# One hybrid decoder layer: the second MLP product summed before its gate, conditioning units dealt out by phase, attention probabilities scaled on ScalarE

## The chip, the cores and the metric

The kernel runs on one core of a Trainium2 chip. The metric is device time in microseconds, median of three runs. Engines are named as the profile names them: PE is TensorE (matmuls; PEld its weight loads), DVE is VectorE, ACT is ScalarE, SP is SyncE, whose queue issues nearly all DMAs.

## What is computed

One layer of a Griffin-like decoder on 256 tokens of width 2048, in float32, cut to what the change touches:

```python
mod = silu(c) @ w_ada + b_ada                     # 6 x 2048 conditioning values
shift1, scale1, gate1, shift2, scale2, gate2 = split(mod, 6)
h = rmsnorm(x) * norm1_g * (1 + scale1) + shift1
lru_x, lru_gate, q, k, v, g_a, g_b = split(h @ w_in)
...
e = exp(logits - m)                               # window 128, sink, 32 heads, 4 kv heads
p = e / (sum(e) + exp(sink - m))
o = p @ v
...
merged = sigmoid(g_a) * y_a + sigmoid(g_b) * y_b
x = x + gate1 * (merged @ w_out)
h2 = rmsnorm(x) * norm2_g * (1 + scale2) + shift2
x = x + gate2 * (relu(h2 @ w_ff1) ** 2 @ w_ff2)   # d_ff = 8192
return rmsnorm(x) * final_g
```

## The kernel before, in words

Everything is kept transposed: 128 features on the partitions, 256 tokens along the row. The work on TensorE is a list of units (`units`). One unit is one block of 128 output features, so up to 16 weight blocks of 128x128; `w_load` fetches its weights by one DMA of up to 1 MB into a `raw` tile (four of them, `RAW_BUFS`, line 260's conditioning rows use the same four), then `w_split` cuts them in chunks of 1024 columns into a rounded part `wh` (ACT, L160) and a remainder `wl` (DVE, L162), with three buffers of each. PE multiplies with both parts: three matmuls for each block in the narrow form (L176, L177, L178), two in the wide form (L189, L190, with a first one at L192). The loop at the end of the builder loads up to two units ahead (`LOOK`), runs a unit, and then takes work from two lists.

The first list is `side`: attention, the recurrence and elementwise work, put there by `later(cost, ...)` and paid from a credit of 2.3 per full unit. For four heads at a time `att_scores` does the score matmuls (L452), the bias, the row maximum (DVE, L457) and the exponentials in place, with their row sums (ACT, L467); `att_values` multiplies the exponentials by the reciprocal of the sum (DVE, L484, eight instructions for each group of four heads), transposes them on PE (L489), copies them out of PSUM (ACT, L491) and multiplies them with v (L496, copied out at L498). There are eight groups.

The second list is the conditioning. `mod` has 96 columns of 128 values; each is one `ada_unit`: a DMA of 1 MB from `w_ada` (SP) and one DVE instruction over 128x2048 with a running sum (L260). The first 32 (shift1, scale1) are done before the units begin. Of the rest 16 give gate1, 16 scale2, 16 shift2 and 16 gate2, in this order. `ada_credit` says when: during the input projection (units before `n_ya`) it grows by 0.45 for each 2048 columns of weights; from there to the unit `n_z`, in which 80 are wanted, by what is left over the units left; after that by 0.3 a unit. Whenever it is above zero one unit is issued and 1 is taken off. A unit of the second MLP product in the first quarter (`ff2_unit`, `c == 0`, L693) asks with `flush(5 * KT + f + 1)` for the column of gate2 that it needs.

The units in order: k and v (2 units of two blocks with 6 of their 16 weight blocks left, since the first ten were done in an earlier pass), q (8 such), the recurrence's x branch (8 such), its gate branch (2 such, then 12 of one block with 10 weight blocks left), the branch gates gA and gB (4 with 10 blocks, 28 full), the two branch projections (32 full), the output projection (16), and then four quarters of the MLP: 16 units of the first product (`ff1_unit`, L675 to L677), 16 of the second (`ff2_unit`). A result of a quarter of the first product is kept as a pair tile of the pool `kp` (49 pair tiles); `ff2_unit` multiplies the two PSUM halves by the column of gate2 and adds them to the residual `x1`, with one DVE instruction for each half, in every quarter. In the last quarter it also takes the squares for the final norm.

Instructions are put on the engines in an order that the Tile scheduler fixes at build time from priorities and modelled times; on the chip each engine takes its queue strictly in that order.

Of the kernel before, what the change touches and what calls it, by code (L numbers as in the profile page):

```python
# [19 lines left out]
KT = 16  # L20
# [13 lines left out]
LAG, CC, CG, CV, CS = 2, 1.0, 0.6, 0.3, 2.5  # L34

ADA_LAST, QUIET_OUT, QUIET_FF1 = 0.3, 2, 3
LOOK, CREDIT, Z_FROM, ADA_RATE, ADA_FIRST = 2, 2.3, 12, 0.45, 0.85

PASSES = [(0, 2, 56), (2, 6, 56), (6, 10, 40)]
NATIVE = {(2, u) for u in range(0, 56, 16)}  # L40
# [16 lines left out]
def hybrid_layer(ctx: ExitStack, tc: tile.TileContext, x, xt, wada, w_p, w_r, w_f, vec, lruw, relb,  # L57
# [19 lines left out]
    def pair(dt=F32):  # L77
        return kp.tile([P, 2, T], dt, tag="k2", name=nm("k"))
# [293 lines left out]
    def later(cost, fn, *a):  # L372
        side.append((cost, fn, a))
# [99 lines left out]
    def att_values(g):  # L473

        kv = g // 2
        ss, dn = ast.pop(g)
        vs = slice(64 * kv, 64 * kv + 64)
        for t in range(2):
            po = bank([P, T])
            pvs = []  # L480
            for i in (2 * t, 2 * t + 1):
                for b, sl in HALVES:
                    c = 2 * i + b
                    ve.tensor_scalar(out=ss[i][:, sl], in0=ss[i][:, sl], scalar1=dn[:, c:c + 1], scalar2=None,  # L484
                                     op0=ALU.mult)
                pt = bank([P, 384])

                for n, j in enumerate((0, 2, 1)):
                    te.transpose(pt[:, n * P:(n + 1) * P], ss[i][:, j * P:(j + 1) * P], idt)  # L489
                pv = tmp([P, 384])  # L490
                se.activation(pv, pt, AF.Copy)  # L491
                pvs.append(pv)

            for kb, cols, pc in ((1, slice(0, 256), slice(0, 256)), (0, slice(128, 256), slice(256, 384))):
                for i in range(2):
                    te.matmul(po[64 * i:64 * i + 64, cols], lhsT=vtok[:, kb, vs], rhs=pvs[i][:, pc],  # L496
                              start=kb == 1, stop=kb == 0)
            se.activation(res[F_Q + 2 * g + t], po, AF.Copy)  # L498
# [170 lines left out]
    def ff1_unit(c, f):  # L669
# [14 lines left out]
            ff[c, f] = split(t[:, 1])  # L684
        add_unit(run)

    def ff2_unit(c, f):
        def run(w):
            if c == 0:
                flush(5 * KT + f + 1)  # L690
            ps = gemm_wide(w, [ff[c, j] for j in range(16)], join=False)
            for i in range(2):
                ve.scalar_tensor_tensor(out=x1[f], in0=ps[:, i], scalar=mod[:, 5 * KT + f:5 * KT + f + 1], in1=x1[f],  # L693
                                        op0=ALU.mult, op1=ALU.add)
            if c == 3:
                if f == 0:
                    stat[3] = sp.tile([P, T], F32, tag="asq", name=nm("asq"), bufs=1)

                if f < 15:
                    sumsq(stat[3], x1[f], f == 0)  # L700
                else:
                    stat[4] = tmp([P, T])
                    se.activation(stat[4], x1[f], AF.Square)
                se.activation(x1[f], x1[f], AF.Copy, scale=vc[:, V_GF + f:V_GF + f + 1])
        add_unit(run)

    def flush(n_ada=0):
        while side:
            _, fn, a = side.pop(0)
            fn(*a)  # L710
        while ada_next[0] < n_ada:
            ada_unit()

# [3 lines left out]
    in_units(F_Q, 16, q_fin)  # L717
    in_units(F_LX, 16, lx_fin)
    in_units(F_LG, 16, lg_fin)
    in_units(F_GA, 16, lambda f, ps, part: branch_gate(F_GA + f, ps, part))  # L720
    in_units(F_GB, 16, lambda f, ps, part: branch_gate(F_GB + f, ps, part))
    n_ya = len(units)
# [15 lines left out]
    for n, (run, src, size, native) in enumerate(units):  # L738
# [11 lines left out]
            credit -= cost  # L750
        left = n_z - n
        if n < n_ya:
            ada_credit += size / 2048 * ADA_RATE
        else:
            ada_credit += max(0, 5 * KT - ada_next[0]) / left if left > 0 else ADA_LAST
        if n_ff1 - QUIET_OUT <= n < n_ff1 or n_ff1 + 16 - QUIET_FF1 <= n < n_ff1 + 16:
# [120 lines left out]
```

## Time and profile before

| | us |
|---|---|
| median of three runs (1599.3 to 1602.97) | 1599.39 |
| the profiled execution's own time | 1599.42 |
| its span, first to last instruction | 1597.6 |
| PE busy in the span | 1560.4 |
| DVE busy | 1223.7 |
| ACT busy | 872.7 |

The page gives the busy time of each engine over the whole span. The view of windows gives the same for any stretch, with the mean granted clock of TensorE and the rate of the DMAs; the view of waits gives the idle time of an engine and the instruction that ended it; the timeline gives single instructions in order of time. On PE an instruction's busy time is longer than its spacing, since matmuls are pipelined.

### The profile page before, as it was taken

Reading aid. Unit: us, or ns where it says so; the run is one execution under the profiler, and the core shown is the slowest. Engines: PE = TensorE matmul, PEld = TensorE weight load, DVE = VectorE, ACT = ScalarE, POOL = GpSimd, SP = SyncE. Lnnn points to the kernel's source line nnn. Section 1 sums busy time; section 2 is a strip of 40 time slices with the busy share of each in tenths; the row PEclk is TensorE's granted clock in tenths of the full one; section 3 lists DMA queues with packets and bytes.
Section 4 is the critical chain, followed back from the end, with each engine's and each line's share of the span. In section 5 each row is a group of like instructions: output and inputs, shape, how many; then the busy total and the mean of one; then the engine's idle time right before and its main releaser. Section 6 shows DMA issues by size and latency. Waiting matters only on the chain.

```text
span 1597.6 us, 26576 instructions
## 1 busy us (share of the span) xinstructions
PE 1560.4 (98%) x10684; PEld 1434.8 (90%) x10684; DVE 1223.7 (77%) x1970; ACT 872.7 (55%) x1421; POOL 0.2 (0%) x4
## 2 busy tenths in 40 slices
PE   5999999999999999999999999999999999999997
PEld 4999998899988888888889998899989998899987
DVE  7798998898989879788898667865665556655665
ACT  5733447686886564445465553355434553355554
POOL 0000000000000000000000000000000000000000
PEclk7999999999999999999999999999999999999999
DMA  8898976557767768787886666865555555555552
GB/s 322 325 345 324 338 272 208 201 191 238 287 237 280 265 244 310 277 297 292 323 302 245 237 237 243 332 242 185 185 184 185 185 185 184 185 185 185 185 186 78
DMA packets 61707, 387.99 MB, mean 243 GB/s; under 512 B 6576, under 2 KB 11024, under 8 KB 19216
## 3 DMA queue, kind: packets, MB, share of 16 engines
q1 hardware_dynamic: 57168, 381.95, 66.7%
q10 hardware_dynamic: 4416, 4.35, 0.9%
q8 instruction: 83, 1.36, 0.3%
q14 instruction: 40, 0.33, 0.1%
HBM read 384.13 MB, written 2.15 MB: 242 GB/s over the span
## 4 chain that ended last, share of the span: by engine, by line
PE 88%; DVE 5%; ACT 2%; DMA 2%; issue 2%; SPq 0%; ACTq 0%; DVEq 0%
PE pg L190 32%; PE pg L189 15%; PE pg L676 8%; PE pg L675 8%; PE pg L677 8%; PE pg L178 4%; PE pg L176 4%; PE pg L177 4%; DVE wl L162 2%; DMA ra<-in_wada_dram 1%; PE pg L205 1%; PE pg L192 1%; DVE ra L260 1%; ACT wh L160 1%; PE pa L489 1%
## 5 line engine op out<-in xcount | busy, mean ns | idle before, releaser
L160 ACT ACTIVATE wh<-rw 128x1024 fp32r<-128x1024 f32 (+2 forms) x534 | 545.4, 1024 | 612.4 <-PE pg L190 318.0
L162 DVE TENSOR_TENSOR wl<-rw,wh 128x1024 fp32r<-128x1024 f32 (+2 forms) x534 | 628.2, 1178 | 241.7 <-ACT wh L160 235.7
L190 PE MATMUL pg<-k,wh 128*128 128x512 f32 x2240 | 776.4, 396 | 0.3 <-DVE k L142 0.3
L189 PE MATMUL pg<-k,wl 128*128 128x256 f32 x2100 | 589.4, 281 | 0.2 <-DVE wl L162 0.2
L190 PEld LDWEIGHTS pg<-k,wh 128*128 128x128 f32 x2240 | 412.5, 188 | 86.4 <-PE pg L190 0.6
L189 PEld LDWEIGHTS pg<-k,wl 128*128 128x128 f32 x2100 | 397.0, 189 | 7.2 <-DVE wl L162 0.6
L676 PE MATMUL pg<-z,wh 128*128 128x256 f32 x1024 | 290.6, 284 | 0.0
L675 PE MATMUL pg<-z,wh 128*128 128x258 f32 x1024 | 289.7, 283 | 0.0
L677 PE MATMUL pg<-z,wl 128*128 128x258 f32 x1024 | 289.7, 283 | 0.0
L176 PE MATMUL pg<-k,wh 128*128 128x256 f32 x832 | 237.4, 287 | 10.9 <-ACT k L141 9.0
L178 PE MATMUL pg<-k,wl 128*128 128x256 f32 x832 | 234.0, 284 | 3.0 <-DVE wl L162 2.8
L177 PE MATMUL pg<-k,wh 128*128 128x256 f32 x832 | 235.1, 283 | 0.2 <-DVE k L142 0.2
L260 DVE CUSTOM_DVE_ANT_0 ra<-ra,scr,vc 128x2048 f32<-128x2048 f32 x96 | 225.1, 2346 | 12.1 <-DMA ra<-in_wada_dram 12.0
L677 PEld LDWEIGHTS pg<-z,wl 128*128 128x128 f32 x1024 | 195.3, 191 | 0.0
L675 PEld LDWEIGHTS pg<-z,wh 128*128 128x128 f32 x1024 | 195.1, 190 | 0.0
L676 PEld LDWEIGHTS pg<-z,wh 128*128 128x128 f32 x1024 | 194.3, 190 | 0.2
L176 PEld LDWEIGHTS pg<-k,wh 128*128 128x128 f32 x832 | 157.5, 190 | 13.9 <-ACT k L141 9.5
L178 PEld LDWEIGHTS pg<-k,wl 128*128 128x128 f32 x832 | 157.2, 190 | 5.2 <-DVE wl L162 4.0
L177 PEld LDWEIGHTS pg<-k,wh 128*128 128x128 f32 x832 | 157.8, 190 | 1.2 <-DVE k L142 0.5
L693 DVE SCALAR_TENSOR_TENSOR k<-pg,mod,k 128x256 f32<-128x256 f32 x128 | 61.8, 484 | 31.3 <-PE pg L190 29.2
L192 PE MATMUL pg<-k,wl 128*128 128x256 f32 x140 | 39.6, 283 | 2.1 <-DVE wl L162 2.1
L679 DVE TENSOR_REDUCE sh<-pg 128x1 f32<-128x2 f32 x64 | 10.2, 159 | 38.4 <-PE pg L677 38.4
(154 smaller groups left out, 983.5 us busy)
## 6 DMA issues: line engine op xcount, KB each, us to landing
rw<-in_w_f_dram SPq DMA_DIRECT2D x204, 1024.0 KB, 4.9
ra<-in_wada_dram SPq DMA_DIRECT2D x96, 1024.0 KB, 6.2
rw<-in_w_p_dram SPq DMA_DIRECT2D x31, 1024.0 KB, 6.0
rw<-in_w_r_dram SPq DMA_DIRECT2D x20, 768.0 KB, 4.9
rw<-in_w_r_dram SPq DMA_DIRECT2D x16, 640.0 KB, 3.9
bt<-ud ACTq DMA_DIRECT2D x8, 512.0 KB, 4.2
xt<-in_xt_dram SPq DMA_DIRECT2D x8, 256.0 KB, 5.0
lw<-in_lruw_dram SPq DMA_DIRECT2D x4, 512.0 KB, 5.7
```

The source lines that it names most:

```text
L160: se.activation(wh[:, :c], raw[:, o:o + c], AF.Copy)
L162: ve.tensor_tensor(out=wl[:, :c], in0=raw[:, o:o + c], in1=wh[:, :c].bitcast(F32), op=ALU.subtract)
L176: te.matmul(ps, lhsT=wh[:, w], rhs=hl[:, 0], start=k == 0, stop=False)
L177: te.matmul(ps, lhsT=wh[:, w], rhs=hl[:, 1], start=False, stop=False)
L178: te.matmul(ps, lhsT=wl[:, w], rhs=hl[:, 0], start=False, stop=k == n - 1)
L189: te.matmul(ps[:, 0], lhsT=wl[:, w], rhs=hl[:, 0], start=False, stop=False)
L190: te.matmul(ps, lhsT=wh[:, w], rhs=hl, start=k == 0, stop=k == n - 1)
L260: r = ve.tensor_tensor_reduce(out=raw, in0=raw, in1=scr, scale=1.0, scalar=vc[:, V_BADA + c:V_BADA + c + 1], op0=ALU.mult, op1=ALU.add, ac ...
L675: te.matmul(ps, lhsT=wh[:, e], rhs=z[k][:, 0:258], start=k == 0, stop=False)
L676: te.matmul(ps[:, 0:256], lhsT=wh[:, e], rhs=z[k][:, 258:514], start=False, stop=False)
L677: te.matmul(ps, lhsT=wl[:, e], rhs=z[k][:, 0:258], start=False, stop=k == KT - 1)
L693: ve.scalar_tensor_tensor(out=x1[f], in0=ps[:, i], scalar=mod[:, 5 * KT + f:5 * KT + f + 1], in1=x1[f], op0=ALU.mult, op1=ALU.add)
```

## The change

Three edits. In `att_values` the multiplication by the reciprocal of the sum (L484) becomes an ACT Copy with a scale for each partition, in place as before. In the unit loop `ADA_RATE` (0.45 for 2048 columns) goes; in its place the credit grows by `ADA_BUSY` = 0.12 a unit, whatever the unit's size, up to the first unit of the branch gates (`n_ga`), and by `ADA_GATES` = 0.55 a unit from there to `n_ya`. In `ff2_unit` the first three quarters are summed without the gate in eight new pair tiles `acc` of the pool `kp`: the first quarter writes them (ACT copies one PSUM half, DVE adds the other), the second and third add both halves; a side task `gate2_sum`, put on the list in the third quarter, multiplies the sum by gate2 into `x1`; the last quarter does what every quarter did. The flush that asked for gate2 column by column in the first quarter becomes `flush_ada(6 * KT)` in the first `gate2_sum`.

```diff
-LOOK, CREDIT, Z_FROM, ADA_RATE, ADA_FIRST = 2, 2.3, 12, 0.45, 0.85
+LOOK, CREDIT, Z_FROM, ADA_FIRST = 2, 2.3, 12, 0.85
+
+ADA_BUSY, ADA_GATES = 0.12, 0.55
...
-                    ve.tensor_scalar(out=ss[i][:, sl], in0=ss[i][:, sl], scalar1=dn[:, c:c + 1], scalar2=None,
-                                     op0=ALU.mult)
+                    se.activation(ss[i][:, sl], ss[i][:, sl], AF.Copy, scale=dn[:, c:c + 1])
...
+    acc, accp = {}, {}
+
+    def gate2_sum(f):
+        if f == 0:
+            flush_ada(6 * KT)
+        ve.scalar_tensor_tensor(out=x1[f], in0=acc[f], scalar=mod[:, 5 * KT + f:5 * KT + f + 1], in1=x1[f],
+                                op0=ALU.mult, op1=ALU.add)
+
     def ff2_unit(c, f):
         def run(w):
+            ps = gemm_wide(w, [ff[c, j] for j in range(16)], join=False)
             if c == 0:
-                flush(5 * KT + f + 1)
-            ps = gemm_wide(w, [ff[c, j] for j in range(16)], join=False)
-            for i in range(2):
-                ve.scalar_tensor_tensor(out=x1[f], in0=ps[:, i], scalar=mod[:, 5 * KT + f:5 * KT + f + 1], in1=x1[f],
-                                        op0=ALU.mult, op1=ALU.add)
+                if f % 2 == 0:
+                    accp[f // 2] = pair()
+                acc[f] = accp[f // 2][:, f % 2]
+                se.activation(acc[f], ps[:, 1], AF.Copy)
+                ve.tensor_tensor(out=acc[f], in0=ps[:, 0], in1=acc[f], op=ALU.add)
+            elif c < 3:
+                for i in range(2):
+                    ve.tensor_tensor(out=acc[f], in0=ps[:, i], in1=acc[f], op=ALU.add)
+            if c == 2:
+                later(0.5, gate2_sum, f)
             if c == 3:
+                for i in range(2):
+                    ve.scalar_tensor_tensor(out=x1[f], in0=ps[:, i], scalar=mod[:, 5 * KT + f:5 * KT + f + 1],
+                                            in1=x1[f], op0=ALU.mult, op1=ALU.add)
...
+    n_ga = len(units)
...
-            ada_credit += size / 2048 * ADA_RATE
+            ada_credit += ADA_BUSY if n < n_ga else ADA_GATES
```

## Rows read from the trace of the kernel before

**Rows 1.** The page, part 1: busy time of each engine in the span, share, instructions.
```profile
PE 1560.4 (98%) x10684; PEld 1434.8 (90%) x10684; DVE 1223.7 (77%) x1970; ACT 872.7 (55%) x1421; POOL 0.2 (0%) x4
```

**Rows 2.** The view of windows: from and to, length, then busy time (and instructions) of PE, PEld, DVE, ACT and POOL, granted clock of TensorE as a share of full speed, busy share of the DMA engines, GB/s. In order: the start, the first passes, k and v, attention, the recurrence, the last of the recurrence beside the first branch gates, the other branch gates, the projections, the first MLP quarter's first and second product, the other quarters, the end.
```profile
0.00:40.00 40.00, 21.67 (x86) 16.61 (x87) 28.84 (x50) 20.71 (x40) 0.20 (x4) 0.74 0.87 322
...
220.00:240.00 20.00, 19.18 (x163) 18.29 (x162) 19.47 (x60) 7.84 (x14) 0.00 (x0) 1.00 0.62 228
240.00:340.00 100.00, 96.98 (x815) 85.20 (x814) 86.88 (x286) 73.61 (x220) 0.00 (x0) 1.00 0.58 198
340.00:405.00 65.00, 62.20 (x506) 61.16 (x505) 60.29 (x113) 49.45 (x88) 0.00 (x0) 1.00 0.69 233
405.00:460.00 55.00, 52.67 (x321) 47.11 (x320) 48.42 (x78) 46.68 (x75) 0.00 (x0) 0.97 0.74 270
460.00:600.00 140.00, 139.69 (x796) 121.61 (x795) 121.00 (x181) 94.54 (x177) 0.00 (x0) 1.00 0.73 261
600.00:860.00 260.00, 260.00 (x1500) 228.03 (x1500) 227.85 (x344) 131.00 (x192) 0.00 (x0) 1.00 0.80 293
...
955.00:1045.00 90.00, 90.00 (x531) 79.39 (x530) 74.29 (x83) 33.99 (x33) 0.00 (x0) 1.00 0.79 294
1045.00:1585.00 540.00, 540.00 (x3794) 506.69 (x3793) 325.45 (x443) 272.23 (x362) 0.00 (x0) 1.00 0.52 180
1585.00:1598.00 13.00, 4.45 (x41) 4.13 (x39) 4.23 (x11) 3.91 (x8) 0.00 (x0) 0.86 0.44 161
```

**Rows 3.** The view of PE's waits, asked for five stretches from 220 us to 600 us: which matmul waited, for what, total us, times, longest us.
```profile
PE pg L176 <- DVE kd L407: 0.8, 1, 0.8
...
PE pa L489 <- DVE as L457: 2.1, 3, 1.0
PE pa L452 <- DVE k L501: 0.5, 1, 0.5
...
PE pg L178 <- DVE wl L162: 2.8, 2, 1.8
...
PE pg L192 <- DVE wl L162: 2.1, 1, 2.1
PE pg L189 <- DVE wl L162: 0.2, 1, 0.2
```

**Rows 4.** The timeline of DVE at three places (360, 386 and 442 us): start, length, engine, line, instruction, count.
```profile
360.30 2.34 DVE L260 CUSTOM_DVE_ANT_0 ra<-ra,scr,vc 128x2048 f32<-128x2048 f32 x1
...
362.57 1.55 DVE L162 TENSOR_TENSOR wl<-rw,wh 128x1024 fp32r<-128x1024 f32 x2
...
385.85 2.35 DVE L260 CUSTOM_DVE_ANT_0 ra<-ra,scr,vc 128x2048 f32<-128x2048 f32 x1
...
442.55 2.35 DVE L260 CUSTOM_DVE_ANT_0 ra<-ra,scr,vc 128x2048 f32<-128x2048 f32 x1
...
445.43 2.34 DVE L162 TENSOR_TENSOR wl<-rw,wh 128x1024 fp32r<-128x1024 f32 x2
```

**Rows 5.** The timeline of PE after the wait at 446.7 us, and the window of half clock: the matmuls L190 and L189 in turn, first at half clock, then at full; then the window with columns as in Rows 2.
```profile
446.68 0.39 PE L192 MATMUL pg<-k,wl 128*128 128x256 f32 x1 [2.08 <-DVE wl L162]
...
449.29 0.63 PE L190 MATMUL pg<-k,wh 128*128 128x512 f32 x1
...
449.93 0.63 PE L190 MATMUL pg<-k,wh 128*128 128x512 f32 x1
...
451.37 0.40 PE L190 MATMUL pg<-k,wh 128*128 128x512 f32 x1
...
451.72 0.40 PE L190 MATMUL pg<-k,wh 128*128 128x512 f32 x1
...
447.40:450.80 3.40, 3.40 (x13) 2.92 (x12) 3.40 (x9) 2.13 (x3) 0.00 (x0) 0.50 1.00 376
```

**Rows 6.** The view of windows for the instructions of line L260 alone (two records each): stretch, length, DVE busy.
```profile
240.00:340.00 100.00, 10.91 (x10) 1.00 0.58 198
340.00:405.00 65.00, 9.41 (x8) 1.00 0.69 233
405.00:460.00 55.00, 9.43 (x8) 0.97 0.74 270
460.00:600.00 140.00, 25.89 (x22) 1.00 0.73 261
955.00:1045.00 90.00, 23.56 (x20) 1.00 0.79 294
```

**Rows 7.** The view of lines from 219 us to 340 us, shapes apart: the probabilities' multiplication as it is, on DVE; then the same stretch from 240 us to 340 us in the view of windows for line L484 alone.
```profile
L484 DVE TENSOR_SCALAR t<-t,as 128x256 f32<-128x256 f32 x32 | 11.1, 347 | 0.0
...
L484 DVE TENSOR_SCALAR t<-t,as 128x128 f32<-128x128 f32 x32 | 9.0, 281 | 0.1
...
240.00:340.00 100.00, 16.21 (x64) 1.00 0.58 198
```

**Rows 8.** The timeline of ACT in one group of exponentials (in place, a bias for each partition, each followed by the read of its sum); then, from the view of lines over the whole span, ACT's Copy with a scale for each partition at the end of the kernel: count, busy us, mean ns of one, idle before.
```profile
260.26 0.49 ACT L467 ACTIVATE t<-t,as 128x256 f32<-128x256 f32 x1
260.66 0.19 ACT L467 ACTIVATION_READ_ACCUMULATOR t<-t,as 128x1 f32 x1
260.76 0.39 ACT L467 ACTIVATE t<-t,as 128x128 f32<-128x128 f32 x1
261.05 0.19 ACT L467 ACTIVATION_READ_ACCUMULATOR t<-t,as 128x1 f32 x1
...
L704 ACT ACTIVATE k<-k,vc 128x256 f32<-128x256 f32 x16 | 8.2, 510 | 0.5
```

**Rows 9.** The view of ACT's waits from 240 us to 340 us, and then of SP's from 240 us to 460 us (columns as in Rows 3).
```profile
ACT t L491 <- PE pa L489: 10.1, 7, 2.6
ACT as L463 <- DVE as L462: 6.2, 6, 1.5
...
SPq L152 <- DVE mod L260: 20.9, 5, 6.6
```

**Rows 10.** The view of lines over the whole span, shapes apart: instructions of the kinds that the new sum uses.
```profile
L196 ACT ACTIVATE t<-pg 128x256 f32<-128x256 f32 x76 | 27.7, 364 | 0.0
...
L693 DVE SCALAR_TENSOR_TENSOR k<-pg,mod,k 128x256 f32<-128x256 f32 x128 | 61.8, 484 | 31.3 <-PE pg L190 29.2
L197 DVE TENSOR_TENSOR t<-pg,t 128x256 f32<-128x256 f32 x76 | 31.7, 417 | 0.0
```

More of the change, by code (lines that the diff above doesn't have):

```diff
@@ L710, in flush, with flush_ada @@
             fn(*a)
+        flush_ada(n_ada)
+    def flush_ada(n_ada):
         while ada_next[0] < n_ada:
```

## Prediction

> **What bounds the kernel now.** I read the page's first part, then the busy time of each engine by stretches, then PE's waits stretch by stretch, and last single instructions around the longest waits. PE is busy 1560.4 of 1597.6 us [rows 1], so at most 37 us of idle time can be won, plus what a low clock costs. The windows show where that idle time lies [rows 2]: 18.3 us in the first 40 us, 8.5 us in the last 13 us, and 0.8 + 3.0 + 2.8 + 2.3 + 0.3 = 9.3 us between 220 and 600 us. From 600 to 860 us and from 955 to 1585 us it is zero. The change touches neither the start nor the end: its earliest edit acts from the first unit of the input projection on (220 us), its latest in the last MLP quarter, where the instructions stay as they are. So the gain has to come from 9.3 us, and a loss can come from anywhere.
>
> What ends PE's waits in 220 to 600 us is DVE in every row [rows 3]: the remainder of the weights (wl, L162) in the recurrence (2.8 us in two waits) and at the first gates (2.1 and 0.2 us), the attention's row maxima and q sums in attention (2.6 us). Three of the four longest waits have the same picture on DVE's queue [rows 4]: a conditioning instruction (L260, 2.35 us, nearly twice a wl instruction of 1.2 us) begins at 360.3, 385.9 and 442.6 us, the wl that PE needs is behind it, and PE stands for 1.8, 1.0 and 2.1 us. After the last of these the granted clock is 0.50 of 2.4 GHz for 3.4 us [rows 5]: two successive L190 start 0.64 us apart there and 0.35 us apart after it, so 3.4 us did the work of 3.4 x 0.35 / 0.64 = 1.9 us and 1.5 us were lost. The other waits of this region were followed by no fall of the clock [rows 2]. Altogether 10.8 us lie in reach.
>
> **The change part by part. Conditioning by phase.** The credit before grew by 0.45 x (20 x 0.75 + 12 x 0.625) = 10.1 over the 32 units ahead of the branch gates, so ten or eleven conditioning units were issued there; after it grows by 32 x 0.12 = 3.8, so four are, at about the 1st, 9th, 17th and 26th unit. By busy time over 2.35 us, 4.6 lie in 240 to 340 us, 4 in 340 to 405, and 4 + 11 in 405 to 600 [rows 6]. After, I count one in attention, two in the recurrence (some 345 and 390 us) and 0.55 x 32 = 17.6 in the branch gates. DVE loses 3.6 x 2.35 = 8.5 us of work in attention and 4.7 us in the recurrence and gains 2.6 x 2.35 = 6 us in the gates, where it is busy 169.4 of 195 us now and would be 175.5, 90% [rows 2].
>
> In the recurrence the wait behind the unit at 360 us goes (-1.8 us); the one at 386 us (-1.0) may come back, since a unit still falls near 390 us: I take half. Together -2.3 us, bounds -2.8 and 0. Next in line there is ACT, busy 49.5 of 65 us, with no wait of PE to its name in this region. At the gates the first four units are short (10 of 16 weight blocks), and the new rate has no size in it: 0.55 each, so three conditioning units stand in the first four gate units where two stood (0.28 each). A unit more in 20 us at 2.35 us of DVE and 1 MB of DMA: 270 GB/s would be 320, below the 376 that the DMAs moved at full share [rows 2, 5]. So the wait at 446.7 us and its clock loss (3.6 us together) may go, since one conditioning unit less stands right there, or be bought anew some places earlier: bounds -3.6 and +3.6 (a second such wait with its clock). I take half of it as gone, -1.8 us, because the number of units from 405 to 460 us stays near four. On SP each conditioning DMA takes one of the four raw tiles from the weights: weight loads waited 20.9 us for L260 to free one [rows 9]. Six fewer of them there can only bring weights earlier; no PE wait ends on a DMA, so nothing is counted.
>
> From 600 us on the spread to the 80th unit corrects itself: 26.6 conditioning units instead of some 24 over 44 units, 3 x 2.35 = 7 us more of DVE in about 240 us, where it is busy 88% and PE never waits [rows 2]. That cover would go only if DVE came close to full.
>
> **Probabilities on ACT.** Sixty-four multiplications leave DVE: 16.2 us of its time between 240 and 340 us [rows 7]. On ACT no such instruction stands in attention. The nearest in kind is L704, a Copy with a scale for each partition, in place, 0.51 us for 256 columns, with no table load on its line; the nearest in place are the exponentials on the same tiles, 0.49 us for 256 and 0.39 for 128 [rows 8]. From the start of one to the start of its successor these take 0.40 and 0.29 us, so 32 x 0.40 + 32 x 0.29 = 22.1 us; the upper bound is whole lengths, 32 x (0.51 + 0.39) = 28.8 us, the lower is the DVE price, 16.2. I take 22.1, since ACT's instructions overlap like this all through the stretch. So in 240 to 340 us DVE goes from 86.9 to 86.9 - 16.2 - 8.5 = 62 us and ACT from 73.6 to 95.7 of 100 us [rows 2]. The bound changes hands: ACT is now as full as PE is (97.0). ACT's new instruction waits for the reciprocal of its group (DVE); behind it in ACT's queue stand the copies of the transposes (L491, already waiting 10.1 us for PE) and the rounding of weights (L160), for which wl and then PE wait. The order on PE is fixed, so a late transpose holds up weight matmuls too.
>
> A rule of the Trainium skill speaks against this edit. The Trainium skill's page "VectorE: DVE Perf Modes" (Mode 2x_2P, and the row on placement in Specifications) says that a float32 operation with one tensor source, in SBUF on both sides, runs at two elements a cycle on VectorE, and that VectorE sits closer to SBUF, ScalarE to PSUM. The trace agrees: the same tiles cost 16.2 us on DVE [rows 7] and some 22.1 us on ACT [rows 8]. By the rule alone the work is moved to the dearer engine and would better stay where it is: without this edit its -0.6 us below falls away and the sum would be -4.1.
>
> Price on the path: for two heads four multiplications stand ahead of PE's transposes. On DVE they take 16.2 / 16 = 1.0 us, on ACT 22.1 / 16 = 1.4, so the chain of each of the 16 pairs grows by 0.4 us: between 0 (hidden under weight matmuls) and 6.4 us if each is waited for. PE waited for DVE ahead of transposes three times [rows 3]; I take five of 16, +2.0 us. Against this the 2.6 us of waits for DVE in attention should go, since DVE has 38 us of air instead of 13. Attention together -0.6 us, bounds -3.4 (with the 0.8 at 231 us) and +6.4.
>
> **The second MLP product.** In the first quarter two instructions of 0.48 us on DVE become one of 0.36 on ACT and one of 0.42 on DVE; in the second and third two of 0.48 become two of 0.42 [rows 10]; 16 further ones of about 0.48 come in the third quarter. DVE is busy 74 of 90 us in the first of these stretches and 325 of 540 after it, ACT 34 and 272 [rows 2]; PE has no idle time there, and the PSUM buffer that waits for the eviction comes round only after three more units of 5.6 us. All of this is hidden, at 0. Ten conditioning units stand in the first quarter's second product [rows 6]; at 0.3 a unit it keeps about five, and the rest go on to about 1125 us, beside units that need 180 GB/s [rows 2]. That relieves stretches in which PE did not wait: 0. The eight tiles of the sum leave 49 - (8 residual + 16 input + 16 squares + 8) = 1 pair tile to spare. The first squares of the second quarter therefore wait for tiles of the first, which are freed by second-product matmuls that PE has passed before the unit that writes them; queued behind such a wait would be ACT's weight rounding, but it ends before it begins. If that cover went (PE running the first product of the next quarter ahead of the last second products), it would cost up to one unit, 5.6 us.
>
> **The sum.** Against the profiled execution's own 1599.42 us, which is the median of the runs (1599.39) to 0.03: attention -0.6, recurrence -2.3, gates -1.8, the rest 0, together -4.7. That makes 1594.7, or -0.29%.
>
> **The rivals.** S, ACT takes DVE's place in attention: ACT's 95.7 us of work would have to fit in 100 us, but it also stood 6.2 us for DVE's maxima and 10.1 us for transposes [rows 9], and such waits can't all be filled from a queue in fixed order. If two thirds of these 16.3 us stay, the stretch needs 95.7 + 10.9 = 106.6 us: +6.6; with the work that is pushed into the recurrence, where ACT had the tables to reload, and one more fall of the clock (+1.5), about +8; nothing gained at the gates, -2.3 kept in the recurrence: 1605. It decides from the point where ACT's idle share in attention falls under about 5%. For it: the full ACT. Against it: half of the idle time on ACT is waiting for DVE work that now comes sooner.
>
> B, all waits that DVE ends between 220 and 600 us go, and the clock stays up: -9.3 - 1.5 = -10.8, 1588.6. For it: DVE's load falls from 89% to 71% over 240 to 405 us [rows 2]. Against it: ACT.
>
> N, the waits only move: a conditioning unit stands in front of some wl wherever it is put, and what DVE gives ACT takes: 1599.4.
>
> G, the dense start of the gates: three conditioning units in the first four gate units, DVE standing on their DMA with wl behind: one wait of 2.1 us and one low clock of 1.5 more than now, and the recurrence's gain gone into it: 1599.4 + 3.6 + 0 = 1603.
>
> **How the numbers follow.** What a measurement of this kernel can tell from no change is about 0.3%, 4.8 us; so faster means under 1594.6 and slower over 1604.2. Forecast (1591 to 1599): 0.42, of which 0.22 lie under 1594.6. B: 0.20. N: 0.16. S: 0.14, of which 0.12 over 1604.2. G: 0.08, of which 0.04 over 1604.2. Faster 0.22 + 0.20 = 0.42; slower 0.12 + 0.04 = 0.16; within 0.42. The range is 1588 to 1606: it takes in B, leaves out the outer half of S and what is beyond B.
>
> **What would show it.** The line of ACT with 64 copies of 128x128 and 128x256 at some 0.39 and 0.49 us, starts 0.29 and 0.40 apart; DVE at some 62 and ACT at some 95 us in attention; L260 with one or two instructions in attention, two in the recurrence, 17 or 18 in the gates, the last near 1125 us; no wait behind L260 near 360 us; PE without idle time from 600 us to 1585 us. Wrong it would be if PE's waits in attention end on ACT (S), if a new wait with half clock stands near 410 to 450 us (G), or if any idle time shows after 955 us (tiles of the pool).

## The result, and the profile after

After: 1606.13 us (median of 6 runs, 1605.79 to 1608.34); before, on the same chip: 1602.27 (6 runs, 1599.30 to 1605.10). The ratio is 1.0029, interval [1.0017, 1.0041]: slower by about 0.3%, some 4.7 us, where 0.3% faster was forecast. The profiled execution took 1606.55 us, its span is 1604.0 against 1597.6.

The page of after, part 1 [rows 1]:

```profile
PE 1563.6 (97%) x10684; PEld 1435.1 (89%) x10684; DVE 1203.5 (75%) x1906; ACT 901.8 (56%) x1505; POOL 0.2 (0%) x4
```

DVE has 64 instructions fewer, ACT 84 more (64 copies, 16 of the new sum and 4 more table loads). The view of windows of after, columns as in [rows 2]: attention, the recurrence, the first gates, the other gates, the projections, two parts of the MLP:

```profile
240.00:340.00 100.00, 95.77 (x762) 80.83 (x761) 54.63 (x192) 86.94 (x271) 0.00 (x0) 0.98 0.44 140
340.00:405.00 65.00, 64.47 (x514) 62.98 (x513) 59.73 (x117) 54.10 (x98) 0.00 (x0) 1.00 0.62 207
405.00:460.00 55.00, 54.51 (x356) 49.53 (x355) 52.45 (x83) 47.65 (x76) 0.00 (x0) 1.00 0.78 290
460.00:600.00 140.00, 136.10 (x761) 117.58 (x759) 123.72 (x185) 95.54 (x173) 0.00 (x0) 0.99 0.78 281
600.00:860.00 260.00, 260.00 (x1489) 227.50 (x1488) 234.42 (x348) 131.81 (x199) 0.00 (x0) 1.00 0.82 302
...
955.00:1045.00 90.00, 90.00 (x521) 78.75 (x520) 58.19 (x62) 39.05 (x51) 0.00 (x0) 1.00 0.71 256
1045.00:1585.00 540.00, 540.00 (x3817) 507.13 (x3816) 339.92 (x467) 274.19 (x364) 0.00 (x0) 1.00 0.55 190
```

In attention PE looks almost as busy as before (95.77 for 96.98 us), but 762 matmuls lie there instead of 815, and its weight loads are busy 80.83 us instead of 85.20 [rows 2]: time is lost that the busy column does not show. The recurrence and the first gates are cleaner than before (64.47 and 54.51 of 65 and 55 us, for 62.20 and 52.67). From 460 to 600 us 3.9 us of idle time have come where 0.3 stood.

PE's waits of after, from 235 to 342 us and from 342 to 600 us, columns as in [rows 3]:

```profile
PE pa L490 <- ACT t L486: 2.4, 2, 1.6
PE pa L490 <- DVE as L459: 0.9, 4, 0.3
PE pg L178 <- ACT wh L162: 0.8, 1, 0.8
...
PE pg L194 <- DVE wl L164: 1.8, 2, 1.3
PE pg L192 <- DVE k L144: 1.2, 1, 1.2
PE pg L192 <- ACT wh L162: 0.8, 1, 0.8
PE pg L178 <- ACT wh L162: 0.5, 1, 0.5
```

In attention two transposes (L490) now wait for the new ACT copies (L486); of the recurrence's waits one of 0.5 us is left, at 342.3 us and for ACT's rounding (wh, L162), and the one of 2.1 us at 446.7 us is gone. New are a wait of 1.2 us for DVE's k (L144) at 594.6 us, ahead of the first projection, where 0.3 us stood before [rows 3], and three waits between 482 and 491 us, on the timeline of PE (in brackets the idle time before the matmul and what ended it):

```profile
482.59 0.39 PE L194 MATMUL pg<-k,wl 128*128 128x256 f32 x1 [0.49 <-DVE wl L164]
...
488.98 0.50 PE L192 MATMUL pg<-k,wh 128*128 128x512 f32 x1 [0.76 <-ACT wh L162]
490.82 0.39 PE L194 MATMUL pg<-k,wl 128*128 128x256 f32 x1 [1.34 <-DVE wl L164]
```

The half clock now stands in two places, the second right behind these waits. The view of windows:

```profile
277.00:280.40 3.40, 3.40 (x19) 2.78 (x18) 2.35 (x5) 2.85 (x15) 0.00 (x0) 0.50 0.81 234
492.10:495.50 3.40, 3.40 (x12) 2.88 (x11) 3.40 (x6) 2.40 (x4) 0.00 (x0) 0.50 0.75 253
```

Where the 6.4 us of span come from is read by taking the same matmul in two traces and subtracting its start. The last column is e4 below, the change without the ACT copies:

| stretch | forecast | after - before | e4 - before |
|---|---|---|---|
| start to first score matmul (234.8 us) | 0 | +0.13 | +0.92 |
| to the first wide matmul (421.3): attention, recurrence | -2.9 | +5.75 | -1.56 |
| to wide matmul 128 (474.0): the wait at 446.7 and its half clock | -1.8 | -3.75 | -3.74 |
| to wide matmul 192 (496.4) | 0 | +4.93 | +3.36 |
| to the projections (586.5) | 0 | +0.97 | +0.77 |
| to the MLP (855.5) | 0 | +0.09 | +0.10 |
| to the end (1597.6) | 0 | -1.76 | -1.78 |
| sum | -4.7 | +6.36 | -1.93 |

Two things failed: attention, and the stretch in front of wide matmul 192. The two columns differ by 5.75 + 1.56 = 7.3 us up to the first wide matmul, and after it only by the half clock at 492 us: 4.93 - 3.36 = 1.6. Of the 7.3 us the half clock at 277 us is some 1.5. e1, below, takes as long from the first score to the last P V matmul (105.0 us against 105.2) at a clock of 1.00; its half clock before the first wide matmul lies at 398.8 us, in the recurrence.

### The profile page after: what moved, and what is told of

Read it like the earlier page. It is cut to its first block, busy times and chain, and to the rows that moved or that the text cites. A ratio compares the mean times of both kernels' runs of the same rounds, so it can differ in the third digit from the quotient of the medians.

```text
span 1604.0 us, 26627 instructions
## 1 busy us (share of the span) xinstructions
PE 1563.6 (97%) x10684; PEld 1435.1 (89%) x10684; DVE 1203.5 (75%) x1906; ACT 901.8 (56%) x1505; POOL 0.2 (0%) x4
## 4 chain that ended last, share of the span: by engine, by line
PE 89%; DVE 4%; ACT 4%; DMA 2%; issue 2%; SPq 0%; ACTq 0%; DVEq 0%
PE pg L192 29%; PE pg L191 14%; PE pg L676 8%; PE pg L678 8%; PE pg L677 8%; PE pg L180 6%; PE pg L178 6%; PE pg L179 5%; PE pg L207 2%; DVE wl L164 1%; ACT wh L162 1%; PE pa L497 1%; PE pg L194 1%; DMA ra<-in_wada_dram 1%; DVE ra L262 1%
## 5 line engine op out<-in xcount | busy, mean ns | idle before, releaser
L162 ACT ACTIVATE wh<-rw 128x1024 fp32r<-128x1024 f32 (+2 forms) x534 | 544.4, 1023 | 598.8 <-PE pg L192 315.9
L262 DVE CUSTOM_DVE_ANT_0 ra<-ra,scr,vc 128x2048 f32<-128x2048 f32 x96 | 225.0, 2346 | 7.0 <-DMA ra<-in_wada_dram 6.8
L708 DVE TENSOR_TENSOR k<-pg,k 128x256 f32<-128x256 f32 x64 | 27.2, 425 | 16.4 <-PE pg L192 15.3
```

What stands on the lines that cost most here:

```text
L162: se.activation(wh[:, :c], raw[:, o:o + c], AF.Copy)
L262: r = ve.tensor_tensor_reduce(out=raw, in0=raw, in1=scr, scale=1.0, scalar=vc[:, V_BADA + c:V_BADA + c + 1], op0=ALU.mult, op1=ALU.add, ac ...
```

## The experiments

All ratios are to runs of the kernel before on the same chip, with the 95% interval; in five rounds each. "Before" is the kernel before, "change" the changed kernel.

### The three edits one by one

e1, before with this edit alone:

```diff
-                    ve.tensor_scalar(out=ss[i][:, sl], in0=ss[i][:, sl], scalar1=dn[:, c:c + 1], scalar2=None,
-                                     op0=ALU.mult)
+                    se.activation(ss[i][:, sl], ss[i][:, sl], AF.Copy, scale=dn[:, c:c + 1])
```

> Only the probabilities' scaling moves to ScalarE; conditioning and MLP sum as before. Theory A (ScalarE becomes the bound in attention): ScalarE busy 94 to 97 of 100 us in 240 to 340 us, new PE waits that end on the scaling copies or on the weight rounding of ScalarE, +3 to +8 us against before. Theory B (the loss of the whole change comes from the conditioning units in the branch gates, the scaling is neutral): -2 to +1 us. Theory C (the loss is a matter of the order that the scheduler happens to find, no edit has a price of its own): any sign, with the waits at other places than behind the scaling copies.

e2, before with the credit by phase alone:

```diff
-            ada_credit += size / 2048 * ADA_RATE
+            ada_credit += ADA_BUSY if n < n_ga else ADA_GATES
```

> Only the conditioning is dealt out by phase (0.12 a unit, then 0.55); scaling on VectorE and gate2 column by column as before. Theory A: the waits behind conditioning instructions in the recurrence go, some -3 to -6 us. Theory B: a wait of 1 to 3 us and 3.4 us of half clock stand in the gates near 440 to 500 us as in the changed kernel, 0 to +4 us. Either way VectorE loses about 8 us of work in 240 to 340 us.

e3, before with the sum of the second MLP product alone (`ff2_unit`, `gate2_sum`, `flush_ada` as in the change):

> Only the second MLP product is summed without its gate; scaling and conditioning rates as before. All theories: within 0.1% of before, no PE idle time after 600 us; the conditioning instructions end near 1130 us and not at 1042 us. If the last 1.7 us that the changed kernel gained after 600 us belong to this edit, -1 to -2 us.

e4, the change without the ACT copies (the diff of e1 the other way round):

> The whole change but for the scaling, which stays on VectorE. Theory A: faster than the changed kernel by 3 to 8 us, so -4 to +1 us against before. Theory B: as slow as the changed kernel, +3 to +5 us against before, with the half clock near 490 us still there.

| | us | ratio | 240 to 340 us: PE (x), DVE, ACT |
|---|---|---|---|
| e1 | 1608.76 | 1.0051 [1.0038, 1.0064] | 94.66 (x764), 64.06, 86.70 |
| e2 | 1599.10 | 0.9995 [0.9987, 1.0003] | 96.75 (x807), 78.71, 72.87 |
| e3 | 1600.75 | 1.0002 [0.9994, 1.0011] | 96.98 (x814), 87.02, 73.74 |
| e4 | 1598.54 | 0.9991 [0.9982, 0.9999] | 96.77 (x807), 78.73, 72.86 |

The ACT copies alone carry the slowdown (+0.51%, 8.2 us); the other two edits are neutral to slightly good. e4 is a little faster than before, by an interval that ends at 0.9999, and by the ratios 0.38% faster than the change (1.0029 / 0.9991); with g1, below, it is the best version found here. e1 came out just above the 3 to 8 us of theory A, but with ACT at 86.70 us and not the 94 to 97 expected; e2 lies between its two theories.

### ACT's time, or the chain in front of the transposes?

In e1 the copies are both on the chain to PE's transposes and in ACT's queue. f1 keeps the DVE multiplications and adds 64 copies of the same sizes to a tile that nobody reads; f2 leaves the multiplication out; f3 puts it on POOL; f4 moves only the 128-column halves:

```diff
+                    se.activation(junk[:, sl], scr[:, sl], AF.Copy, scale=dn[:, c:c + 1])   # f1: added
...
-                    ve.tensor_scalar(out=ss[i][:, sl], ...)                                 # f2: left out
...
+                    nc.gpsimd.tensor_scalar(out=ss[i][:, sl], ...)                          # f3: instead
...
+                    if b == 0:                                                              # f4
+                        se.activation(ss[i][:, sl], ss[i][:, sl], AF.Copy, scale=dn[:, c:c + 1])
...                                                                             # else on DVE as before
```

> The kernel before, whose VectorE scales the probabilities as it did; beside each of the 64 multiplications ScalarE does a Copy with a scale of the same shape, from a constant tile into a scratch tile that nobody reads. It gives ScalarE the same 22.6 us of work without putting any of it between the exponentials and the transposes. Theory O (the loss of the scaling alone, +8.2 us, is ScalarE's occupancy: weight rounding and copies stand in its queue): +5 to +9 us. Theory L (the loss is the longer chain from the exponentials over the scaling to the transposes on PE, whose order is fixed): 0 to +3 us.

> The kernel before without the 64 multiplications: the probabilities are left unscaled, so the output isn't the layer's. Neither VectorE nor ScalarE has the work. It prices the relief that VectorE gets from giving up the scaling, without ScalarE's side. If VectorE's load is what holds PE in attention: -2 to -5 us. If the relief is worth nothing: -0.5 to +1 us.

> The kernel before with the 64 multiplications on GpSimd, which is idle otherwise. Theory O: ScalarE is not loaded, so no loss of its kind: -3 to +2 us if GpSimd takes less than about 1 us for one. Theory L: GpSimd's instruction stands in the chain as ScalarE's did, so a loss of the same kind or larger: +4 to +12 us.

> The kernel before with the 32 multiplications of 128 columns on ScalarE and the 32 of 256 columns left on VectorE. ScalarE gets 32 x 0.3 = 9.6 us in place of 22.6. Theory O: a loss in proportion or less, 0 to +3.5 us. Theory L: each pair of heads still waits for a ScalarE instruction ahead of its transposes: +4 to +8 us.

| | us | ratio | 240 to 340 us: PE (x), DVE, ACT |
|---|---|---|---|
| f1 | 1611.80 | 1.0064 [1.0051, 1.0078] | 96.17 (x764), 78.54, 87.08 |
| f2 | 1599.55 | 0.9986 [0.9977, 0.9995] | 98.05 (x825), 74.44, 74.39 |
| f3 | 1614.05 | 1.0077 [1.0062, 1.0091] | 89.77 (x721), 64.09, 65.34 |
| f4 | 1605.52 | 1.0020 [1.0010, 1.0031] | 96.83 (x794), 78.85, 82.01 |

Copies that nothing waits for cost 0.64%, 10.3 us; leaving DVE's multiplication out saves 0.14%, 2.2 us. Together +8.1, as much as e1 costs, within intervals of 1.4 to 2.2 us either way. Half the work in f4 (its 32 copies keep ACT busy for 10.5 us, the 64 of the change for 24.3) costs 3.2 us, where 10.5 / 24.3 x 8.2 = 3.5 would be in proportion. So the loss does not need copies on the chain; ACT's time in this stretch is enough. (f1's copies take the reciprocal as their scale, so they too stand in ACT's queue until it is there; ACT waited 1.0 us for that.) Part of the losses is the clock: between 240 and 500 us the profiled executions of e1, f1, f4 and the change have two stretches of half clock of 3.4 us, before one, and e2, e3, e4 and f2 none; one cost some 1.5 us in the prediction's working. f1 lost more than the 5 to 9 us of its theory O. f3 shows that a chain made long enough has a price too, 12.3 us, where theory O gave -3 to +2: POOL takes 968 ns for each of the 64 in the mean, 60.7 us in all, and ten waits of PE's transposes end on it:

```profile
PE pa L489 <- POOL t L484: 8.1, 10, 2.6
```

### ACT's queue, or a new order on TensorE?

The PE idle time of attention explains little of 8 us, and the scheduler lays PE's order anew for each kernel: 454 weight matmuls between the first score and the last P V matmul in e1, 418 before. i1 and i4 are e1 and f1, i3 is the change, with PE's order in that stretch held to that of before (i3: of e4); i2 is before with the order of e1. The edges order and bring no wait; the orders of ACT and DVE were left to the scheduler:

```diff
+    for a, b in zip(PE_ORDER, PE_ORDER[1:]):
+        tc.add_manual_dep(pe_ins[b], f"I-{a}",
+                          mybir.DependencyInfo(mybir.DependencyClass.NoSync, mybir.DependencyReason.DATA),
+                          reason="order of TensorE")
```

> The kernel before with the 64 probability copies on ACT (as e1), but with TensorE's order from the first score matmul to the last P V matmul held, by edges that only order and bring no wait, to that of the kernel before (643 matmuls). Theory Q (ACT's full queue makes TensorE wait): the loss of e1 stays, +8 us or more, now as plain idle time of PE, 1609 or above. Theory O (the order in which the scheduler lays the matmuls at build time, made from its modelled times, is the larger part; e1 has 36 more weight matmuls inside attention and 101 changes of kind against 82): only the idle part stays, +1 to +4 us, 1602 to 1605.

> The kernel before, probabilities scaled on DVE, but with TensorE's order in attention held to that of e1 (679 matmuls). Theory Q: the order by itself costs nothing, 1600 to 1602. Theory O: the order by itself costs most of e1's loss, +4 to +7 us, 1605 to 1608, with no more PE idle time in attention than the kernel before has.

> The whole change, with TensorE's order in attention held to that of the change without the ACT scaling (e4). Theory O: between e4 and the change, nearer to e4, 1600 to 1602. Theory Q: as the change or worse, 1606 or above.

> The kernel before with 64 further ACT copies of the same sizes that nothing waits for (as f1), TensorE's order in attention held to that of the kernel before. Theory Q: +10 us as in f1, 1611. Theory O: f1's loss too came mostly from the order, here +2 to +5 us, 1603 to 1606.

The table is worked out from the matmul records between the first score and the last P V matmul. "Net" is the length less 0.118 us, the usual spacing, for each weight matmul that the order put there; "runs of one kind" counts the runs of successive matmuls of one kind (weights, scores, transposes, P V and so on), one more than the changes; a pair is two P V matmuls that start within 20 ns of each other:

| | us, ratio | length | weight matmuls | net | idle | runs of one kind | P V pairs |
|---|---|---|---|---|---|---|---|
| before | | 93.7 | 418 | 44.4 | 3.0 | 82 | 37 |
| e1 | 1.0051 | 105.0 | 454 | 51.5 | 5.4 | 101 | 30 |
| i1 | 1606.99, 1.0034 [1.0022, 1.0046] | 98.8 | 418 | 49.5 | 6.5 | 82 | 31 |
| f1 | 1.0064 | 104.3 | 451 | 51.1 | 3.8 | 91 | 23 |
| i4 | 1607.87, 1.0039 [1.0026, 1.0051] | 100.9 | 418 | 51.6 | 6.8 | 82 | 31 |
| change | 1.0029 | 105.2 | 454 | 51.6 | 4.2 | 104 | 27 |
| i3 | 1607.46, 1.0035 [1.0023, 1.0047] | 102.7 | 421 | 53.0 | 8.0 | 87 | 28 |
| i2 | 1614.58, 1.0083 [1.0070, 1.0097] | 113.8 | 454 | 60.3 | 11.7 | 101 | 35 |

With the old order most of the loss stays: net +5.1 in i1, +7.2 in i4, and i3 is not faster than the change. What changes is its look: more of it is plain idle time. The window of i1 in attention, and the first of its PE waits there:

```profile
240.00:340.00 100.00, 93.50 (x772) 80.17 (x772) 67.49 (x211) 91.47 (x280) 0.00 (x0) 1.00 0.55 187
```

```profile
PE pa L538 <- ACT t L534: 2.4, 6, 0.9
PE pa L538 <- DVE as L507: 1.6, 3, 1.1
PE pa L545 <- ACT t L540: 1.3, 3, 0.8
```

PE's transposes (L538) wait six times for the ACT copies and its P V matmuls (L545) three times for the copies out of PSUM (L540), which stand behind them on ACT. One such place on the timeline of ACT, ahead of PE's wait of 0.83 us for L540 at 309.79 us: eight probability copies, a rounding, then the copies out of PSUM:

```profile
305.55 2.87 ACT L534 ACTIVATE t<-t,as 128x128 f32<-128x128 f32 x8
308.32 1.04 ACT L210 ACTIVATE wh<-rw 128x1024 fp32r<-128x1024 f32 x1
309.27 0.84 ACT L540 ACTIVATE t<-pa 128x384 f32<-128x384 f32 x2
```

For the change itself (i3, 1606 or above expected) theory Q came out. For i1 and i4 neither theory did: Q gave 1609 and more and 1611, O 1602 to 1605 and 1603 to 1606, and both lie between. The difference of the ratios is 0.17% for e1 and i1 and 0.25% for f1 and i4, each with an uncertainty of some 0.18% (the half intervals in quadrature): of f1's loss a part goes with the order, for e1 it isn't clear of the noise. i2 missed both theories and doesn't settle the order's own price: PE waited 7.8 us in four waits for ACT's copies out of PSUM, an order made for other times.

### The stretch from 474 to 496 us

In e2 and e4 the wait at 446.7 us went too, and 3.4 us were lost again before wide matmul 192. The first theory was the density of conditioning there. g1 is e4 with the old rate in the gates, g2 with 0.25 a unit, g3 with no credit ahead of the gates and the old rate in them:

```diff
+            ada_credit += ADA_BUSY if n < n_ga else size / 2048 * 0.45     # g1; g3 with ADA_BUSY = 0.0
...
+ADA_BUSY, ADA_GATES = 0.12, 0.25                                           # g2
```

> The whole change with the scaling left on VectorE (as in e4_no_scale), but in the branch gates the old rate of 0.45 for 2048 columns in place of 0.55 a unit; 0.12 a unit ahead of them stays. Theory G (the 3.4 us that e4_no_scale loses near 476 to 485 us come from conditioning instructions standing too close there): no wait over 1 us between 405 and 580 us, -4 to -6 us against before. Theory H (they come from ScalarE's table loads, which alternate there between the scan's square roots and the gates' tanh, with one conditioning instruction wherever it falls): the loss stays within 1 us of e4_no_scale, -1 to -3 us against before.

> As e4_no_scale with 0.25 a unit in the branch gates in place of 0.55: eight conditioning units there in place of 17, the rest between 586 and 850 us, where VectorE is busy 90% and would be 97%. Theory G: no loss in the gates, -4 to -6 us against before unless PE begins to wait after 586 us. Theory H: a wait near 480 us still, smaller if no conditioning instruction falls on it, -1 to -4 us.

> As g1_old_gate_rate with 0 in place of 0.12 ahead of the gates: no conditioning instruction in attention and the recurrence at all. It prices what the three that are left there cost: 0 to -2 us against g1_old_gate_rate by both theories.

| | us | ratio | PE waits 470 to 495 us | 600 to 860 us: PE, DVE |
|---|---|---|---|---|
| e4 | 1598.54 | 0.9991 [0.9982, 0.9999] | 0.5, 0.8, 1.3 | no wait |
| g1 | 1600.12 | 0.9991 [0.9983, 1.0000] | 0.6 | 257.19, 236.66 |
| g2 | 1604.63 | 1.0020 [1.0011, 1.0029] | 0.2, 0.7, 1.3 | 256.08, 246.86 |
| g3 | 1605.41 | 1.0025 [1.0016, 1.0033] | 0.6 | 255.81, 241.87 |

g2 has a conditioning instruction at 470.5 us and the next at 495.1 us, none in the nine microseconds ahead of the two longer waits, and these are the same (482.2 and 484.0 us): conditioning at that place is not needed for them. g1 kept its waits under 1 us, as theory G said, but also has fewer table loads there, and its time is that of e4 and not 4 to 6 us under before. What the thinner rates show instead is a sum: what isn't done early is done from 600 to 860 us, and at 236.66 of 260 us of DVE and above PE starts to wait there (2.8, 3.9 and 4.2 us); at the 234.42 of the change it doesn't. g3, expected 0 to 2 us faster than g1, is 0.34% slower: a wait of 2.4 us there came with 6.8 us of half clock.

The second theory was ACT's table loads. On ACT's timeline of after they stand between the roundings of weights (L162) that PE waits for:

```profile
482.13 0.36 ACT L198 ACTIVATE t<-pg 128x256 f32<-128x256 f32 x1
482.51 1.28 ACT L554 ACT_TABLE_LOAD   x1
483.80 0.42 ACT L554 ACTIVATE t<-t 128x256 f32<-128x256 f32 x1
484.24 1.28 ACT L595 ACT_TABLE_LOAD   x1
485.53 0.42 ACT L595 ACTIVATE k<-t 128x256 f32<-128x256 f32 x1
485.96 1.28 ACT L554 ACT_TABLE_LOAD   x1
487.25 0.73 ACT L554 ACTIVATE t<-t 128x256 f32<-128x256 f32 x2
487.88 1.99 ACT L162 ACTIVATE wh<-rw 128x1024 fp32r<-128x1024 f32 x2
```

From 482.5 to 487.9 us ACT does one gate's and the recurrence's functions in turn, three loads of 1.28 us among them, and only then rounds weights; PE waits at 488.98 us. From 470 to 492 us there are six such loads in after, e2, e4 and g2 (3.0 to 3.4 us lost), four in g1 and g3 (some 0.9 us), two in the kernel before. h1 is e4 with the four scans of a group as one side task and the gates' tanh tied to the table of exp; h2 is before and h3 the change with the same:

```diff
-            for i in range(j - 3, j + 1):
-                later(1.0, lru_scan, i)
+            later(4.0, lambda j0: [lru_scan(i) for i in range(j0, j0 + 4)], j - 3)
...
-            se.activation(res[f], ps, AF.Tanh, scale=0.5)
+            table("exp", se.activation(res[f], ps, AF.Tanh, scale=0.5))
```

> As e4_no_scale, with ScalarE's table loads in the last two groups of the recurrence cut down: the four scans of a group are one side task, and the gates' tanh is ordered with the other users of its table. Same arithmetic. Theory K (what e4_no_scale and the changed kernel lose near 476 to 496 us is six table loads of 1.28 us in 16 us on ScalarE, where the kernel before has two): two table loads in that stretch, no wait over 1 us there, -4 to -6 us against before. If conditioning instructions or the order of PE were the cause: -1 to -3 us, as e4_no_scale.

> The kernel before with the same cut of the table loads and nothing else. Theory K: the loss near 470 to 500 us isn't in the kernel before, so only the wait at 446 us, behind five table loads and a conditioning instruction, can shrink: 0 to -4 us.

> The whole change, scaling on ScalarE included, with the same cut of the table loads. Theory K with the occupancy of ScalarE in attention (+7 to +8 us, unchanged): faster than the changed kernel by 3 to 5 us, so -1 to +2 us against before, and still slower than h1_noscale_tables by 5 to 8 us.

Measured: h1 1603.76, 1.0014 [1.0005, 1.0023]; h2 1602.98, 1.0011 [1.0001, 1.0021]; h3 1610.89, 1.0061 [1.0048, 1.0074]. In h1 two loads are left from 470 to 492 us, and wide matmuls 128 to 192 take 23.8 us instead of e4's 25.8 (before 22.4): the loss there fell from 3.4 to 1.4 us. But the scans, now packed, stand on DVE ahead of wl, and PE waits at other places (397.4 and 442.5 us), and still 1.1 us at 484.6 us. The first of PE's waits of h1 from 342 to 600 us:

```profile
PE pg L180 <- DVE wl L164: 2.3, 2, 1.9
PE pg L194 <- DVE wl L164: 1.8, 1, 1.8
PE pg L191 <- DVE wl L164: 1.1, 1, 1.1
```

h2 speaks against the loads: it has two of them from 470 to 492 us, as before has, and still takes 26.3 us for wide matmuls 128 to 192, with a wait of 2.0 us for DVE's wl at 485.6 us and 3.4 us of half clock behind it. So the cause of the loss at this place stays open: fewer loads went with a smaller loss in g1, g3, h1 and h3 (23.4 us instead of 27.4 in the change), but g1 and g3 also moved the conditioning and h1 and h3 the scans, and in h2 the loss came with few loads. This regrouping is no cure: all three kernels became slower than those they came from, where -4 to -6, 0 to -4 and -1 to +2 us against before were expected.

## Why the prediction was wrong, point by point

**Probabilities on ACT: the step that failed.** Its direct price was right: the eight copies from 258.3 us on start 0.29 and 0.40 us apart in turn, as forecast, 22.1 us for 64; in all they keep ACT busy for 24.3 us, where the same work took 16.2 on DVE [rows 7]. The view of lines of after, 240 to 345 us, shapes apart, and the view of windows for line L486 alone:

```profile
L486 ACT ACTIVATE t<-t,as 128x256 f32<-128x256 f32 x32 | 15.9, 498 | 0.0
...
L486 ACT ACTIVATE t<-t,as 128x128 f32<-128x128 f32 x32 | 12.5, 392 | 3.3 <-DVE as L472 3.3
...
240.00:340.00 100.00, 24.33 (x64) 0.98 0.44 140
```

Wrong was "Price on the path": 0.4 us for each of the 16 pairs, five of them waited for, +2.0 with 6.4 as the upper bound, and -2.6 for the DVE waits. As a count of PE's waits for the copies this was near: two waits, 2.4 us. But up to the first wide matmul the change takes 7.3 us more than without the copies (e4), and f1 shows that the loss comes without any copy on the chain. What the sum left out is what stands behind the copies: ACT's queue also carries the exponentials, the copies of the transposes out of PSUM and the rounding of weights, and 24.3 us more in it push these back. From 240 to 340 us ACT stood 10.1 us for PE's transposes before [rows 9] and stands 1.0 us for them after, so it now comes late to them:

```profile
ACT t L492 <- PE pa L490: 1.0, 3, 0.5
```

The relief of DVE is worth 2.2 us (f2), near the 2.6 counted. Rival S had the mechanism and nearly the time: 1605 forecast, and 1.0029 x 1599.42 = 1604.1; its sign, waits of PE in attention that end on ACT, came too. That the time is so near is in part luck, since the loss before wide matmul 192 is not in its sum. Its condition was off, though: it was to decide when ACT's idle share falls under 5%, and the loss is there at 13% (86.94 of 100 us; 95.7 forecast). All 64 copies lie in that stretch, but 271 instructions of ACT and not 220 + 64: as attention grew, 13 others moved out of it. Here an engine that serves several chains in a fixed order cost time with 13% of it still idle.

Wrong too was "The order on PE is fixed". On the chip it is, but it is laid anew at build time: 36 more weight matmuls in e1's attention, 101 runs of one kind for 82. That hid part of the loss: with the old order PE's idle time grows from 5.4 to 6.5 us (e1, i1), from 3.8 to 6.8 (f1, i4) and from 4.2 to 8.0 (change, i3). i1, i3 and i4 put the order back and most or all of the loss stays; how much of the rest of e1 is the order's remains open.

The rule of the Trainium skill's page "VectorE: DVE Perf Modes" (Mode 2x_2P), which spoke against this edit, was borne out: 16.2 us on DVE [rows 7], 24.3 on ACT. By it the edit was to be left out; e4, which does that, ran at 0.9991, forecast by that sum at -4.1 us, and came to -1.4 by its ratio.

**Conditioning in the recurrence: right.** Both waits behind it went, also in e2, and not only the one and a half that were counted. L260's successor L262 starts at 271.3 us once in attention, at 352 and 384 us in the recurrence, 18 times from 405 to 600 us (17.6 forecast), and the last starts at 1126.9 us (1125).

**The gates: right at its place, wrong in sum.** The wait at 446.7 us and its half clock went whole (-3.75 for the -1.8 taken and the -3.6 bound); some 1.5 us of this is the half clock of the profiled execution of before, which e3 with the same wait doesn't have (-1.6 at this place). But the loss before wide matmul 192 takes 3.4 us back, a half clock in this execution 1.5 more, and 1.0 goes after it, in the wait for DVE's k ahead of the first projection: -3.75 + 4.93 + 0.97 = +2.2, inside the bounds of 3.6 either way, and not the -1.8 taken. "Bought anew some places earlier" was the right picture with the wrong place and the wrong cause: the new loss lies later, and no conditioning instruction has to stand there for it (g2); its cause is open. Rival G's place, the dense start, is clean: PE 54.51 of 55 us.

**The projections: right.** From 600 to 860 us L262 takes 7.0 us more of DVE than L260 did (7 forecast), and PE is busy 260.00 of 260. g1 to g3 show where that cover ends.

**The sum of the second product: right, 0.** e3 is 1.0002 [0.9994, 1.0011]; from 955 us to 1585 us PE has no idle time, so the pool's spare tile sufficed. The instructions cost what was taken. The view of lines of after, 955 to 1585 us:

```profile
L708 DVE TENSOR_TENSOR k<-pg,k 128x256 f32<-128x256 f32 x64 | 27.2, 425 | 16.4 <-PE pg L192 15.3
...
L705 DVE TENSOR_TENSOR k<-pg,k 128x256 f32<-128x256 f32 x16 | 6.7, 418 | 0.0
L704 ACT ACTIVATE k<-pg 128x256 f32<-128x256 f32 x16 | 5.9, 366 | 0.0
```

**Open.** The MLP and the end run 1.8 us shorter in the change and in e4, though PE has no wait over 0.2 us there in either. In e2 it is 1.4 us and in e3 0.3, so most of it comes with the conditioning credit; why isn't known. Open too is the cause of the loss from 474 to 496 us.

## What to carry to other kernels

Price work that is handed to another engine by that engine's time in that stretch and by all that stands behind it in its queue, and not only by the chain that the work lies on: test it with the same work added off the chain (f1). Look at matmuls and weight-load time per stretch, not at PE's busy share alone, and expect the order at build time to change when an engine's load does. Side work that is moved is a sum: count what is left over where it lands, and look for the next late engine at the place where a wait goes.

## What the runs showed of the hardware

TensorE's busy time can stay while work is lost: in f1 it is 96.17 of 100 us with 764 matmuls, before 96.98 with 815. The Trainium skill's page "Perfetto Trace Analysis" (Identifying the Most-Contended Engine) says that matmul busy time, since matmuls are pipelined, is no good measure of how near the engine is to its peak, and names the busy share of weight loads as one of two better ones. This trace agrees: 80.55 us in f1 and 80.83 after, 85.20 before [rows 2].

Two P V matmuls, which write different halves of the output partitions, often start within 20 ns of each other: 37 times before, 23 to 31 times in the kernels with 64 more copies on ACT. The others run in turn, their starts 0.04 to 0.27 us apart, and no idle time shows. In before five groups of them begin with a second matmul that starts 0.05 us after the last of the two copies out of PSUM ends; f1 also has groups that run in turn though the copies ended 0.3 us and more earlier, so lateness isn't the only cause.

The half clock doesn't follow each wait of a length: in e3 the same wait of 2.08 us at 447.18 us ended on the same wl, and the 3.4 us from 447.9 us on ran at 1.00; before they ran at 0.50 [rows 5]. The three waits before 485 us in e4 were followed by 10 us at 1.00, the same three in after by 3.4 us at 0.50. On ACT a change of table took the load's 1.28 us alone: the function after it starts 1.29 us after the load does (482.51 to 483.80).
